# A fused mLSTM, attention and gated-mixing block on one Trainium2 core: norm factors and scales on GpSimd, and a load queue in emission order

## The chip, the cores and the metric

One core of a Trainium2 chip runs the whole block in one launch. The metric is device time in microseconds (us). The kernel before takes 1686.43 us, the median of three runs (1686.1 to 1689.79).

The profile's names for the engines are kept: PE is TensorE (matrix products), PEld its weight loads, ACT is ScalarE, DVE is VectorE, POOL is GpSimd, and SP is the engine whose queue issues most DMAs. Each engine works through its own list of instructions in order; semaphores make it wait for the others.

## The reference, cut to what matters

Sequence and width are 1024, all in float32.

```python
h = rmsnorm(x, norm_g)
(a_q, a_k, a_v, a_o, a_z, a_g, b_q, b_k, b_v, b_z, g_a, g_b) = split(h @ w_in)
# branch A: mLSTM, 4 heads of width 256, once forwards and once backwards in time
q, k = silu(depthwise_conv([a_q, a_k]))
h_fw, h_bw = mlstm(q, k, a_v, gates[0], gates[1]), flip(mlstm(flip(q), flip(k), ...))
hm  = rmsnorm(h_fw + h_bw, ml_norm_g)              # over the 256 of each head
y_a = hm * sigmoid(a_o) * silu(a_z)
# branch B: differential attention, 8 heads
y_b = rmsnorm(attention(b_q, b_k, b_v), da_subln_g) * 0.8 * silu(b_z)
# mixing
mix = sigmoid(g_a + gb[0]) * (y_a @ w_branch_a) + sigmoid(g_b + gb[1]) * (y_b @ w_branch_b)
x   = x + mix @ w_out
return rmsnorm(x, final_g)
```

## The kernel before

**Products.** Every float32 operand is split into a high and a low part (tile names end in H and L: `wH`, `wL`, `vH`, `sl_yb`), and a product is three matmuls: high by high, high by low, low by high. ACT makes the high part by a cast, and DVE or POOL the low part by a subtraction.

**Stages.** Projections and gates open the program; the attention of branch B runs to about 1120 us of the profiled span and stores y_b to DRAM; the mLSTM of branch A runs from there to about 1384 and stores y_a; the mixing runs to about 1591; the output product and the last norm end it. Projections of the gates g_a, g_b (`gate_units`) and of the next head's `v` are filled in between as spare work for PE.

**Order.** `build` puts small units of work into a list, in part interleaved by a `Weaver`, and `run` emits them. From the end of the opening on, the call `keep(E.PE)` makes PE execute in the order of emission. The instructions of ACT, DVE, POOL and SP are put in order by the framework's scheduler, from its own model of their times; on the chip this order is fixed.

**mLSTM head (`ml_head`).** A head has 8 blocks of 128 time steps, and a recurrent state for chunks of 256 in each direction. `weigh` scales the transposed k by its weights: `kwH` on ACT (L1081), then `kwL` on DVE (L1082); `kwH` has a single buffer, so the next half's copy waits for this half's `kwL`. `state` multiplies `vH` by `kwH` into a bank T (L127) and adds it to the state `C` (L1105). `split` casts the state to its parts CH and CL. `scores` (L1119 on) makes the decay weights `W`: POOL masks a row of gates with an affine select (L1136, once 128 and once 256 wide in a block), ACT takes the exponential (L1138), and DVE multiplies it by the scores SS and sums `den` (L1139). `t_tile` normalises: `den`, its reciprocal `rr`, and L1183 (ACT) and L1185 (DVE), which write the scaled `W`. `transposes` turns `W` on PE into a bank T, ACT and DVE split it (L1198, L1035), and `pv` multiplies it by v into PO. `pv` also adds the result to `hm` (L1209) and takes its square sum `ssq` (L1210).

**The head's norm.** After its last block, `pv` calls `rsqrt`: five short DVE operations on 128x8 (L140, L148 to L151) around one power on POOL (L147), with tiles `rh_v`, `rh_y`, `rh_w`. `scale` then multiplies the eight 128x256 tiles `hm` by `rh_y` on ACT (L1216). They are emitted among the first blocks of the *next* head. `load_g` brings the stored gates, and `out` transposes `hm` on PE (`T<-hm`), multiplies by `ml_norm_g` and the gates (L1228) and stores y_a. The last head has no next one: its scales and outputs are in `late`, woven with gate projections. The attention's norm calls the same `rsqrt` with `eng` set to POOL.

**Mixing.** `load_y` (L1310) loads a 512 KB block of y_b or y_a into one of two buffers `yraw`, casts it to its high part on ACT (L1314) and subtracts on DVE (L1315) for the low part; the parts lie in slots of the groups `yb` and `r`, the tiles `sl_yb` and `sl_r`. The y_b loads are woven with the last quarters of the gate projections (`rest`), whose results go from ACT's tanh (L837) through the one buffer `gt` to DRAM (L838, a DMA on SP's queue after the opening). `mix_units` runs pass B (`gb`: y_b by `w_branch_b`) and then pass A. For each block of 128 outputs it loads the gate (`tgl`, L1327) and a weight (`raw`, L173), PE multiplies into `pj`, which has two banks (L429), and DVE multiplies by the gate (L1339 in pass B), which frees the bank. The y_a blocks 0 to 3 are loaded during the second half of pass B, and 4 to 7 at its end.

Of the kernel before, what the change touches and what calls it, by code (L numbers as in the profile page):

```python
# [7 lines left out]
F32 = mybir.dt.float32  # L8
# [3 lines left out]
ALU = mybir.AluOpType  # L12
AX = mybir.AxisListType

S = 1024
D = 1024
EPS = 1e-6
NH_A, DH = 4, 256
NH_B = 8
L = 256  # L20
# [25 lines left out]
class Unit:  # L46
# [5 lines left out]
    def __init__(self, cost, fn, keys=(), tag=None, hold=0.0, name=None, after=(), lane=0):  # L52
        self.cost, self.fn, self.keys = cost, fn, keys
        self.tag, self.hold, self.name, self.after, self.lane = tag, hold, name, after, lane
# [55 lines left out]
class Block:  # L110
    def __init__(self, tc, A):
        self.tc, self.nc, self.A = tc, tc.nc, A
        nc = self.nc
        self.v, self.a, self.p, self.t, self.q = nc.vector, nc.scalar, nc.gpsimd, nc.tensor, nc.sync
        self.wt = {}
        self.raws = {}
        self.ml, self.opening, self.ahead, self.terms, self.forms = False, True, False, {}, 0
        self.rs, self.tk, self.loaded = {}, {}, set()
        for n in ("w1", "w2", "wy", "wr"):
            setattr(self, n, _Late(self, "_" + n))  # L120
        self.gc = {}
# [709 lines left out]
    def gate_units(self, seg, i):  # L831
        key = ("w_in", OFF[seg] + 128 * i)
        idx = (0 if seg == "ga" else 8) + i

        def done(half, ps):
            t = self.wpool.tile([128, 512], F32, name="gt", tag="gt")
            self.a.activation(out=t, in_=ps, func=AF.Tanh, scale=0.5, bias=self.gbh[:, idx:idx + 1])  # L837
            (self.a if self.opening else self.q).dma_start(out=self.tg[seg][i][:, half * 512:(half + 1) * 512], in_=t)  # L838
        return sum((self.proj(key, half, lambda ps, half=half: done(half, ps)) for half in range(2)), [])


# [186 lines left out]
    def ml_head(self, n, st):  # L1028


        v, a, p, q, w2 = self.v, self.a, self.p, self.q, self.w2
        gc = self.gc
        row = lambda c: n * NC + c
        loc = {}
# [167 lines left out]
        def pv(tt):  # L1202
            vH, vL = st["v", tt // NB]
            WH, WL = loc.pop(("WT", tt))
            pairs = [(x[:, i, :], y[:, i, 0:DH]) for x, y in ((WH, vH), (WH, vL), (WL, vH)) for i in range(NB)]
            o = self.bank("PO")[:, 0:DH]
            self.mm(o, pairs)
            h = st["h"][tt]
            v.tensor_tensor(out=h, in0=o, in1=h, op=ALU.add)  # L1209
            a.activation(out=o, in_=h, func=AF.Square, accum_out=st["ssq"][:, tt:tt + 1])  # L1210
            if tt == 7:
                loc["rs"] = self.rsqrt(w2, st["ssq"], 1.0 / DH, EPS, "rh")

        def scale(t):
            for t in (t, t + 1):
                a.mul(st["h"][t], st["h"][t], loc["rs"][:, t:t + 1])  # L1216

        def load_g(half):
            for i in range(2):
# [3 lines left out]
        def out(i, half):  # L1223
            ps = self.bank("T")
            for k in range(4):
# [5 lines left out]
        do = lambda f, *x: Unit(0.0, lambda: f(*x))  # L1231
        step = lambda f: lambda *x: [do(f, *x)]
        return dict(k=step(load_k), HL=lambda c: [do(load_parts, seg, c) for seg in ("ak", "aq")], gb=step(load_gb),
                    v=self.v_units("av", n, vv, order=(3, 2, 1, 0)), weigh=step(weigh),
                    state=lambda c, d: [do(state, c, d, i) for i in range(2)], split=step(split), S=step(scores),
                    I=step(t_tile), T=step(transposes), P=step(pv), scale=step(scale), g=step(load_g),
                    O=lambda half: [do(out, i, half) for i in range(2)])

# [68 lines left out]
        return un, prev["O"](0) + prev["g"](1) + prev["scale"](4) + prev["scale"](6) + prev["O"](1)  # L1307


    def load_y(self, src, i, slot):  # L1310
        raw = self.wy.tile([128, S], F32, name="yraw", tag="yraw", bufs=2)
        self.q.dma_start(out=raw, in_=src[i])
        h, l = slot("H"), slot("L")
        self.a.copy(h, raw)  # L1314
        self.v.tensor_tensor(out=l, in0=raw, in1=h.bitcast(F32), op=ALU.subtract)  # L1315
        return h, l

    def slot(self, which, dt=F32R):
        pool, bufs = {"yb": (self.wy, 16), "mb": (self.wy, 8), "r": (self.wr, 16)}[which]
        return pool.tile([128, S], dt, name="sl_" + which, tag=which, bufs=bufs)  # L1320
# [108 lines left out]
    def build(self):  # L1429
# [19 lines left out]
        do = lambda f, cost=0.0: Unit(cost, f)  # L1449
        pool = lambda *x, **k: tc.tile_pool(*x, **k)  # L1450
        with pool(name="const", bufs=1) as self.const, \
# [3 lines left out]
            E, kept = mybir.EngineType, []  # L1455

            def keep(*engines):

                def f():
                    if kept:  # L1460
                        kept.pop().__exit__(None, None, None)
                    if engines:
                        kept.append(tc.manual_schedule(engines=set(engines)))
                        kept[0].__enter__()
                return Unit(0.0, f)
# [18 lines left out]
            gq = [("gb", i) for i in range(8)] + [("ga", i) for i in range(8)]  # L1484
            fill = lambda m: sum((self.gate_units(*gq.pop(0)) for _ in range(m)), [])
# [16 lines left out]
            st3 = {}  # L1502
            w = Weaver()
            w.add(enter("h", "hpool"), enter("tab", "tab", side="right"), enter("tf", "tf", side="right"),
                  enter("p0", "p0", side="right"), banks("ps0", T=6), keep(E.PE, E.Activation, E.DVE, E.Pool), do(begin))
            k = self.PIECES
# [60 lines left out]
            w.add(enter("w2", "w2", side="right"), banks("ps2", T=2, SS=1, PO=1, I=1))  # L1567
            ml, late = self.ml_units([self.ml_head(n, stm[n]) for n in range(NH_A)], fill(2))
            w.add(do(lambda: setattr(self, "ml", True)), *ml)
            rest = fill(len(gq))  # L1570
            cut = len(rest) // 4
            w.add(*rest[:5])
            w.weave(late, rest[5:cut])
            w.add(do(lambda: setattr(self, "ml", False)), leave("ps2", "w2"), enter("wy", "wy", side="right"))
            yb = lambda x: self.slot("yb")
            loads = [do(lambda k=k: st3.__setitem__(("gb", k), self.load_y(self.yb, k, yb)), 1.0) for k in range(8)]
            w.weave(loads, rest[cut:])

            w.add(leave("h"), enter("wr", "wr"))
            passB = self.mix_units("gb", st3)  # L1580
# [1 line left out]
            loads = [do(lambda k=k: st3.__setitem__(("ga", k), self.load_y(self.ya, k, r)), 1.0) for k in range(4)]  # L1582
            w.add(*passB[:len(passB) // 2])
            w.weave(loads, passB[len(passB) // 2:])
            w.add(*[do(lambda k=k: st3.__setitem__(("ga", k), self.load_y(self.ya, k, yb))) for k in range(4, 8)])
            passA = self.mix_units("ga", st3)
            loads = [do(lambda k=k: self.load_wo(k, st3, "yb"), 1.0) for k in range(3)]
            k = len(passA) // 2
# [52 lines left out]
```

## Time and profile before

| | |
|---|---|
| median of three runs | 1686.43 us |
| the profiled execution's own time | 1687.36 us |
| its span in the profile | 1685.6 us |
| mean granted clock | 0.999 |

| stretch of the span, us | PE busy | ACT | DVE | POOL |
|---|---|---|---|---|
| 0 to 110, opening | 97.59 | 59.32 | 69.72 | 67.30 |
| 110 to 1120, projections and attention | 1004.36 | 479.80 | 644.88 | 456.63 |
| 1120 to 1384, mLSTM | 251.55 | 147.83 | 162.65 | 67.11 |
| 1384 to 1591, gates and mixing | 204.88 | 54.05 | 80.89 | 39.81 |
| 1591 to 1685.6, output | 87.37 | 19.33 | 34.22 | 4.35 |

The profile page gives one execution: how long each engine was busy, which waits it had and what ended them, and the DMAs. A wait is written as the waiting engine and its operation, then `<-` and the engine and operation that released it. An idle time of PE is the difference between a stretch and its busy time; in the mLSTM it is 264.0 - 251.55 = 12.5 us, in the mixing 207.0 - 204.88 = 2.1 us.

### The profile page before, as it was taken

How to read it: one execution, taken by the hardware profiler on the slowest of the kernel's cores; microseconds unless marked ns; L12 is line 12 of the kernel's file. 1: busy time of each engine (PE TensorE's matmuls, PEld its weight loads, DVE VectorE, ACT ScalarE, POOL GpSimd, SP SyncE). 2: the span in 40 equal slices, each digit the busy share in tenths (PEclk: the TensorE clock that was granted, in tenths of full speed). 3: DMA queues.
4: the chain of work that ended last, by engine and by line, in shares of the span. 5: the costliest groups of instructions: out<-in, count | busy, mean ns of one | idle time of the engine just before them, and what ended most of it. 6: DMA issues, size and time to landing. Idle time of an engine off the chain costs nothing. (4 is left out here: it accounts for less than half of the span.)

```text
span 1685.6 us, 25370 instructions
## 1 busy us (share of the span) xinstructions
PE 1645.8 (98%) x9431; PEld 1385.3 (82%) x9431; DVE 992.4 (59%) x1799; ACT 760.3 (45%) x1522; POOL 635.2 (38%) x712
## 2 busy tenths in 40 slices
PE   7999999999999999999999999999999999999998
PEld 5777887887877988898888888899999877888887
DVE  5778678675286766666666665325666754135533
ACT  7454555553255454444445445334655644122221
POOL 5767676655343334333451332122322412212000
PEclk9999999999999999999999999999999999999999
DMA  5334434434231213211322222166455337344222
GB/s 180 101 117 137 138 113 137 126 125 127 74 80 48 74 38 88 51 51 39 100 59 56 62 58 70 57 181 176 144 160 161 89 117 244 126 149 126 88 93 83
DMA packets 175630, 178.79 MB, mean 106 GB/s; under 512 B 12185, under 2 KB 135410, under 8 KB 175506
## 3 DMA queue, kind: packets, MB, share of 16 engines
q1 hardware_dynamic: 174594, 175.58, 34.8%
q8 instruction: 74, 1.21, 0.3%
q10 hardware_dynamic: 912, 1.59, 0.2%
q14 instruction: 50, 0.41, 0.1%
HBM read 114.11 MB, written 46.24 MB: 95 GB/s over the span
## 5 line engine op out<-in xcount | busy, mean ns | idle before, releaser
L429 PE MATMUL pj<-hH,wH 128*128 128x512 f32 x640 | 265.8, 415 | 3.3 <-ACT f L542 1.5
L429 PE MATMUL pj<-hH,wL 128*128 128x512 f32 x640 | 251.3, 393 | 1.8 <-POOL wL L207 1.8
L429 PE MATMUL pj<-hL,wH 128*128 128x512 f32 x640 | 250.1, 391 | 0.2 <-DVE hL L580 0.2
L209 POOL TENSOR_TENSOR wL<-raw,wH 128x1024 fp32r<-128x1024 f32 x41 | 99.7, 2432 | 278.0 <-ACT wH L204 268.3
L928 ACT ACTIVATE e<-S,nm 128x1024 f32<-128x1024 f32 x128 | 142.7, 1115 | 134.1 <-DVE nm L926 133.9
L948 DVE TENSOR_TENSOR pL<-T,pH 128x512 fp32r<-128x512 f32 x128 | 87.9, 688 | 117.4 <-ACT pH L947 116.7
L926 DVE TENSOR_REDUCE nm<-S 128x1 f32<-128x1024 f32 x128 | 150.5, 1217 | 10.1 <-PE S L923 9.3
L451 PE MATMUL pj<-wH,hH 128*128 128x256 f32 x512 | 149.9, 293 | 1.6 <-DVE vL L1035 1.4
L429 PEld LDWEIGHTS pj<-hH,wH 128*128 128x128 f32 x640 | 120.4, 188 | 37.7 <-issue 14.1
L451 PE MATMUL pj<-wL,hH 128*128 128x256 f32 x512 | 144.9, 283 | 1.4 <-POOL wL L207 1.4
L429 PEld LDWEIGHTS pj<-hH,wL 128*128 128x128 f32 x640 | 120.1, 188 | 30.2 <-POOL wL L207 3.4
L451 PE MATMUL pj<-wH,hL 128*128 128x256 f32 x512 | 144.5, 282 | 0.0
L429 PEld LDWEIGHTS pj<-hL,wH 128*128 128x128 f32 x640 | 120.7, 189 | 18.2 <-DVE hL L580 0.6
L429 PE MATMUL pj<-sl_yb,wH 128*128 128x512 f32 x384 | 118.9, 390 | 2.1 <-DVE sl_mb L1339 1.6
L947 ACT CAST pH<-T 128x512 fp32r<-128x512 f32 x128 | 74.7, 584 | 100.5 <-PE T L131 99.8
L204 ACT CAST wH<-raw 128x1024 fp32r<-128x1024 f32 x56 | 58.8, 1050 | 114.7 <-PE pj L429 75.8
L923 PE MATMUL S<-kst,qq 64*128 64x512 f32 x768 | 106.5, 408 | 0.0
L451 PEld LDWEIGHTS pj<-wH,hH 128*128 128x128 f32 x512 | 97.7, 191 | 6.8 <-issue 3.9
L451 PEld LDWEIGHTS pj<-wL,hH 128*128 128x128 f32 x512 | 97.5, 190 | 2.3 <-POOL wL L207 2.3
L451 PEld LDWEIGHTS pj<-wH,hL 128*128 128x128 f32 x512 | 97.7, 191 | 0.1
L934 DVE SCALAR_TENSOR_TENSOR e<-e,r,e 128x1024 f32<-128x1024 f32 x64 | 88.9, 1389 | 2.2
L923 PEld LDWEIGHTS S<-kst,qq 64*128 64x128 f32 x768 | 67.8, 184 | 26.2 <-issue 10.5
(358 smaller groups left out, 4101.4 us busy)
## 6 DMA issues: line engine op xcount, KB each, us to landing
raw<-in_w_in_dram SPq DMA_DIRECT2D x88, 512.0 KB, 3.9
kst<-hl SPq DMA_DIRECT2D x64, 128.0 KB, 2.4
qq<-hl SPq DMA_DIRECT2D x64, 128.0 KB, 2.4
x<-in_x_dram SPq DMA_DIRECT2D x8, 512.0 KB, 6.2
cak<-y SPq DMA_DIRECT2D x16, 256.0 KB, 2.3
cakH<-cin SPq DMA_DIRECT2D x16, 256.0 KB, 4.4
cakL<-tz SPq DMA_DIRECT2D x16, 256.0 KB, 4.1
gm<-oz SPq DMA_DIRECT2D x16, 256.0 KB, 2.8
```

The lines of the kernel that those rows point to most:

```text
L204: self.a.copy(wH, raw)
L209: self.p.tensor_tensor(out=wL, in0=raw, in1=wHf, op=ALU.subtract)
L429: self.t.matmul(ps, lhsT=l[:, k, :], rhs=r, start=(n == 0), stop=(n == 23))
L451: self.t.matmul(ps[:, i, :], lhsT=l, rhs=r[:, k, :], start=(kh == 0 and k == 0 and m == 0), stop=(kh == 1 and k == 3 and m == 2))
L923: self.t.matmul(ps[:, o], lhsT=qq[r, x, c], rhs=k[r, y, o], start=(m == 0), stop=(m == 2))
L926: v.tensor_reduce(out=nm, in_=ps, axis=AX.X, op=ALU.max, negate=True)
L928: a.activation(out=e, in_=ps, func=AF.Exp, bias=nm[:, 0:1], accum_out=Z[:, j, t:t + 1])
L934: v.scalar_tensor_tensor(out=e0, in0=e, scalar=r[:, 0:1], in1=e0, op0=ALU.mult, op1=ALU.add)
L947: a.copy(pH[:, :, s], ps)
L948: v.tensor_tensor(out=pL[:, :, s], in0=ps, in1=pH[:, :, s].bitcast(F32), op=ALU.subtract)
```

## The change

It has two parts.

*The mLSTM's norm.* All of `rsqrt` for a head goes to POOL (`eng=p`). The eight scales of heads 0 to 2 become `tensor_scalar` multiplications on POOL; those of the last head stay on ACT. Nothing else of the head is edited.

```diff
             if tt == 7:
-                loc["rs"] = self.rsqrt(w2, st["ssq"], 1.0 / DH, EPS, "rh")
+                loc["rs"] = self.rsqrt(w2, st["ssq"], 1.0 / DH, EPS, "rh", eng=p)
 
         def scale(t):
             for t in (t, t + 1):
-                a.mul(st["h"][t], st["h"][t], loc["rs"][:, t:t + 1])
+                if n + 1 < NH_A:
+                    p.tensor_scalar(out=st["h"][t], in0=st["h"][t], scalar1=loc["rs"][:, t:t + 1], scalar2=None, op0=ALU.mult)
+                else:
+                    a.mul(st["h"][t], st["h"][t], loc["rs"][:, t:t + 1])
```

*The queue and the loads.* From the mixing on, SP too keeps the order of emission. The eight y_b loads are emitted ahead of the last gate projections instead of being woven with them. `load_y` by default loads straight into the slot of the low part, and the subtraction is done in place; y_a's blocks 4 to 7 keep the way through `yraw`. The stores of the gates go to ACT's DMA queue from a flag `last` on, which a unit at the head of `rest` sets; since `rest` is one unit longer, `rest[:5]` holds one piece of a gate projection fewer ahead of `late`.

```diff
-            (self.a if self.opening else self.q).dma_start(out=self.tg[seg][i][:, half * 512:(half + 1) * 512], in_=t)
+            (self.a if self.opening or self.last else self.q).dma_start(out=self.tg[seg][i][:, half * 512:(half + 1) * 512], in_=t)
...
-    def load_y(self, src, i, slot):
-        raw = self.wy.tile([128, S], F32, name="yraw", tag="yraw", bufs=2)
-        self.q.dma_start(out=raw, in_=src[i])
-        h, l = slot("H"), slot("L")
+    def load_y(self, src, i, slot, direct=True):
+
+        if direct:
+            h, l = slot("H"), slot("L")
+            raw = l.bitcast(F32)
+            self.q.dma_start(out=raw, in_=src[i])
+        else:
+            raw = self.wy.tile([128, S], F32, name="yraw", tag="yraw", bufs=2)
+            self.q.dma_start(out=raw, in_=src[i])
+            h, l = slot("H"), slot("L")
...
-            rest = fill(len(gq))
+            rest = [do(lambda: setattr(self, "last", True))] + fill(len(gq))
...
-            w.weave(loads, rest[cut:])
+            w.add(keep(E.PE, E.SP), *loads, *rest[cut:])
...
-            w.add(*[do(lambda k=k: st3.__setitem__(("ga", k), self.load_y(self.ya, k, yb))) for k in range(4, 8)])
+            w.add(*[do(lambda k=k: st3.__setitem__(("ga", k), self.load_y(self.ya, k, yb, False))) for k in range(4, 8)])
```

Behind the edits the line numbers are larger by 3 (L1216 is L1219 for ACT's scale and L1217 for POOL's, L1228 is L1231) and by 9 from `slot` on (L1314, L1315, L1327 and L1339 are L1323, L1324, L1336 and L1348); a direct load is at L1318. PE's list is the same but for three products, which move behind the last head's transpositions of `hm`.

The scheduler moves more than the edits say. POOL's list at the first change of heads, where head 0's norm meets head 1's first blocks; `-` is before, `+` the change, and the numbers in tile names only tell buffers apart:

```order
 L1136 AFFINE_SELECT W_12377<-gb 128x128
+L140 TENSOR_SCALAR rh_v<-ssq 128x8
 L147 TENSOR_TENSOR rh_y<-rh_v,mhalf 128x8
+L148 TENSOR_TENSOR rh_w<-rh_y 128x8
+L149 TENSOR_TENSOR rh_w<-rh_w,rh_v 128x8
+L150 TENSOR_SCALAR rh_w<-rh_w 128x8
+L151 TENSOR_TENSOR rh_y<-rh_y,rh_w 128x8
+L1217 TENSOR_SCALAR hm<-hm,rh_y 128x256 x7
 L1136 AFFINE_SELECT W_12383<-gb 128x256
+L1217 TENSOR_SCALAR hm<-hm,rh_y 128x256
```

The five DVE operations of the norm and seven of the eight scales now stand between the block's two selects.

ACT's list at the same place, with the exponentials of those two selects (L1138):

```order
 L1179 ACTIVATE hm<-I,al 128x256
 L1138 ACTIVATE W_12377<-W_12377,gc_negM 128x128
-L1216 ACTIVATE hm<-hm,rh_y 128x256 x3
-L1198 CAST WH<-T 128x256
-L1081 ACTIVATE kwH<-T,gc_ws 128x256
+L1198 CAST WH<-T 128x256
 L1138 ACTIVATE W_12383<-W_12383,gc_negM 128x256
-L1216 ACTIVATE hm<-hm,rh_y 128x256
-L1081 ACTIVATE kwH<-T,gc_ws 128x256
-L1060 CAST vH<-pj 128x2x256
-L1216 ACTIVATE hm<-hm,rh_y 128x256
+L1081 ACTIVATE kwH<-T,gc_ws 128x256 x2
```

The scales leave ACT, and the first copy to `kwH`, which stood ahead of the wide exponential, now stands behind it.

DVE's list at the start of pass B, from the last head's outputs on, before:

```order
L1228 SCALAR_TENSOR_TENSOR gA<-T,mlg,gA 128x512 x4
L1315 TENSOR_TENSOR sl_yb<-yraw,sl_yb 128x1024 x8
L1315 TENSOR_TENSOR sl_r<-yraw,sl_r 128x1024 x2
L1339 SCALAR_TENSOR_TENSOR sl_mb<-tgl,pj 128x512
L1315 TENSOR_TENSOR sl_r<-yraw,sl_r 128x1024 x2
L1339 SCALAR_TENSOR_TENSOR sl_mb<-tgl,pj 128x512 x14
```

and with the change:

```order
L1231 SCALAR_TENSOR_TENSOR gA<-T,mlg,gA 128x512 x4
L1324 TENSOR_TENSOR sl_yb<-sl_yb 128x1024 x8
L1348 SCALAR_TENSOR_TENSOR sl_mb<-tgl,pj 128x512 x5
L1324 TENSOR_TENSOR sl_r<-sl_r 128x1024
L1348 SCALAR_TENSOR_TENSOR sl_mb<-tgl,pj 128x512 x2
L1324 TENSOR_TENSOR sl_r<-sl_r 128x1024
```

y_a's first subtraction stood ahead of the first operation that frees PE's bank, and now stands behind five of these.

More of the change, by code (lines that the diff above doesn't have):

```diff
@@ L117, in __init__ @@
         self.ml, self.opening, self.ahead, self.terms, self.forms = False, True, False, {}, 0
-        self.rs, self.tk, self.loaded = {}, {}, set()
+        self.rs, self.tk, self.loaded, self.last = {}, {}, set(), False
         for n in ("w1", "w2", "wy", "wr"):
```

## The prediction

> **What bounds the kernel now.** I read the page's busy shares first, then PE's waits stage by stage, then the timeline at the few places that hold them. Engines go by the page's names: PE is TensorE, ACT ScalarE, DVE VectorE, POOL GpSimd, SP the queue that issues most DMAs.
>
> ```profile
> span 1685.6 us, 25370 instructions
> PE 1645.8 (98%) x9431; PEld 1385.3 (82%) x9431; DVE 992.4 (59%) x1799; ACT 760.3 (45%) x1522; POOL 635.2 (38%) x712
> ```
>
> PE is busy for 98% of the span, so an edit can only fill or widen PE's gaps. PE's list of waits, for the mLSTM (1130 to 1390 us; two lines that the change doesn't touch left out) and for the mixing (1390 to 1600): what waited, for whom, us in total, times, longest.
>
> ```profile
> PE T L131 <- ACT W L1183: 3.4, 5, 0.8
> PE T L131 <- DVE W L1185: 2.7, 3, 1.8
> PE T L131 <- ACT hm L1216: 1.0, 2, 0.5
> PE PO L127 <- ACT WH L1198: 0.7, 3, 0.3
> PE T L127 <- ACT kwH L1081: 0.4, 2, 0.2
> ```
>
> and in the mixing:
>
> ```profile
> PE pj L429 <- DVE sl_mb L1339: 1.6, 1, 1.6
> PE pj L429 <- DVE sl_yb L1315: 0.4, 2, 0.2
> ```
>
> The change can win some 8 us at most in the first and 2 in the second. ACT and DVE have room, so work taken off them pays only where PE waits for them.
>
> **First change of heads (head 0's norm beside head 1's first tiles).** These rows, of PE, ACT, DVE and POOL in turn, are start, duration, engine, line, tiles.
>
> ```profile
> 1212.93 0.28 PE L127 MATMUL T<-vH,kwH 128*128 128x258 f32 x1
> 1215.11 0.28 PE L127 MATMUL SS<-akH,aqH 128*128 128x256 f32 x1
> 1217.44 0.72 PE L131 MATMUL T<-ident,W 128*128 128x128 f32 x2 [0.75 <-ACT W L1183]
> 1217.91 0.36 PE L451 MATMUL pj<-wH,hH 128*128 128x256 f32 x1
> 1207.12 0.19 ACT L1210 ACTIVATION_READ_ACCUMULATOR PO<-hm 128x1 f32 x1
> 1211.96 0.47 ACT L1081 ACTIVATE kwH<-T,gc_ws 128x256 fp32r<-128x256 f32 x1
> 1212.33 0.50 ACT L1138 ACTIVATE W<-W,gc_negM 128x256 f32<-128x256 f32 x1
> 1213.62 0.48 DVE L1082 SCALAR_TENSOR_TENSOR kwL<-T,gc_ws,kwH 128x256 fp32r<-128x256 f32 x1 [0.68 <-ACT kwH L1081]
> 1217.42 0.35 DVE L1185 SCALAR_TENSOR_TENSOR W<-W,rr,W 128x128 f32<-128x128 f32 x1
> 1207.37 0.29 POOL L1136 TENSOR_SCALAR_AFFINE_SELECT W<-gb 128x128 f32<-128x128 f32 x1 [1.05 <-DVE W L1185]
> 1209.43 0.40 POOL L1136 TENSOR_SCALAR_AFFINE_SELECT W<-gb 128x256 f32<-128x256 f32 x1
> ```
>
> Removed: five small DVE operations and eight ACT scales. Moved: in the new order the 256-wide select stands on POOL behind the whole norm chain and seven scales. The exponential that reads it (L1138) stands on ACT ahead of both kwH copies, so it becomes a wait; behind it queue kwH, vH and CH, and PE's state product waits for kwH. The chain's price is that of the attention's norm, which runs on POOL already:
>
> ```profile
> 624.87 1.68 POOL L147 TENSOR_TENSOR rb_y<-rb_v,mhalf 128x8 f32<-128x8 f32 x1
> 627.48 0.20 POOL L151 TENSOR_TENSOR rb_y<-rb_y,rb_w 128x8 f32<-128x8 f32 x1
> 627.77 0.23 POOL L978 TENSOR_SCALAR rb_y<-rb_y 128x8 f32<-128x8 f32 x1
> ```
>
> From the power to the end of L151 is 627.68 - 624.87 = 2.81 us. No row shows a 128x256 TENSOR_SCALAR on POOL; its price lies between the same operation on 128x8 (0.20 to 0.23 us; more elements can't be shorter) and the two-input operation, 0.50 for 128x128 and 1.29 for 128x512, so about 0.76 for 128x256:
>
> ```profile
> L207 POOL TENSOR_TENSOR wL<-raw,wH 128x128 fp32r<-128x128 f32 x120 | 55.2, 496 | 35.3 <-ACT wH L204 33.2 <-POOL W L1136 2.0
> L865 POOL TENSOR_TENSOR m<-m,hl 128x512 f32<-128x512 f32 x16 | 20.6, 1288 | 66.1 <-DVE hl L863 66.1
> ```
>
> I take 0.42, just above the undisturbed select of the same size and one input (0.40 at 1209.43); 0.20 and 0.76 stay as ends.
>
> The Trainium skill, GPSIMD Engine Reference, section 4.1 (Engine selection), speaks against this part: for elementwise work on a tile it names VectorE, since GpSimd is about half as fast with two inputs and near line rate with one. By its section 3.1, 2.6 cycles an element at 1.2 GHz gives an estimate of 0.55 + 0.2 = 0.75 us a scale and a sum 6 us higher; 1.03 cycles gives 0.42 and this sum. The trace has both rates, not this operation.
>
> Now the sum. POOL's first select ends at 1207.66 and the last square sum is there at 1207.31. The first norm operation (0.23 and a gap of 0.08) starts at 1207.7, the power at 1208.0, L151 ends at 1210.8, seven scales (2.9) at 1213.8, the select at 1214.2. ACT's next operation followed the exponential by 0.40 before, so kwH starts at 1214.65, 2.7 later than 1211.96. Then kwH, kwL, kwH come one after the other (each half's kwL reads what the next kwH overwrites), 0.47 + 0.48 + 0.46 + 3 x 0.05, and the second kwL starts at 1216.2, 2.6 later than 1213.62. PE came to the scores (SS) 1.5 us after it, so at 1217.7, and would be at the transposition of W 1.4 later, 1219.1. But DVE's L1185 came 3.8 us after that kwL, and what stands between them still adds up to some 3.7 us: 1219.9 + 0.35, and PE goes on at 1220.4 instead of 1217.91. **+2.5 us**, with today's waits for WH (0.3) and W (0.75) already spent in it. The second change of heads has the same rows 61.5 us later: **+2.5**.
>
> **Third change of heads.** Here POOL gets three scales ahead of the narrow select and one more ahead of the wide one.
>
> ```profile
> 1331.44 0.44 PE L131 MATMUL T<-ident,W 128*128 128x128 f32 x2 [1.80 <-DVE W L1185]
> 1335.97 0.28 PE L127 MATMUL SS<-akH,aqH 128*128 128x256 f32 x1
> 1329.09 1.64 POOL L147 TENSOR_TENSOR rh_y<-rh_v,mhalf 128x8 f32<-128x8 f32 x1
> 1331.46 0.29 POOL L1136 TENSOR_SCALAR_AFFINE_SELECT W<-gb 128x128 f32<-128x128 f32 x1 [0.74 <-DVE rh_w L150]
> 1334.50 0.47 DVE L1082 SCALAR_TENSOR_TENSOR kwL<-T,gc_ws,kwH 128x256 fp32r<-128x256 f32 x1
> ```
>
> The 1.80 us wait goes, since DVE no longer stands still for the power. What is late next is kwH: the chain ends at 1332.1, three scales at 1333.4, the narrow select at 1333.75, its exponential lets kwH start at 1334.1, the second kwL at 1335.6 instead of 1334.50. The scores come 1.1 later, the next W 0.2 more: **+1.3 us** net.
>
> **Last head.** Its scales stay on ACT, its chain goes to POOL, and three products (0.68 us) slip behind the transpositions of hm.
>
> ```profile
> 1380.12 3.31 ACT L1216 ACTIVATE hm<-hm,rh_y 128x256 f32<-128x256 f32 x8 [1.91 <-DVE rh_y L151]
> ```
>
> The sum of squares is there at 1376.46, so the chain ends at 1379.63 and the scales start 0.44 earlier; they are what PE waits for, so 0.68 - 0.44 = **+0.2 us**.
>
> **Mixing.** yb goes straight into the slot of its low part, SP issues in emission order, and six gate stores go to ACT's queue.
>
> ```profile
> 1423.69 0.61 PE L429 MATMUL pj<-sl_yb,wH 128*128 128x512 f32 x2
> 1424.14 0.39 PE L429 MATMUL pj<-sl_yb,wL 128*128 128x512 f32 x1
> 1426.14 0.73 PE L429 MATMUL pj<-sl_yb,wH 128*128 128x512 f32 x2 [1.61 <-DVE sl_mb L1339]
> 1431.48 0.39 PE L429 MATMUL pj<-sl_yb,wL 128*128 128x512 f32 x1
> 1431.99 0.50 PE L429 MATMUL pj<-sl_yb,wH 128*128 128x512 f32 x1
> 1424.26 1.23 DVE L1315 TENSOR_TENSOR sl_r<-yraw,sl_r 128x1024 fp32r<-128x1024 f32 x1 [2.38 <-ACT sl_r L1314]
> 1425.40 0.68 DVE L1339 SCALAR_TENSOR_TENSOR sl_mb<-tgl,pj 128x512 f32<-128x512 f32 x1
> yraw<-yb SPq DMA_DIRECT2D x8, 512.0 KB, 4.1
> tgb<-gt ACTq DMA_DIRECT2D x6, 256.0 KB, 2.0
> ```
>
> DVE subtracts ya's low part in front of the L1339 that frees PE's bank. In the new order five L1339 stand ahead of the first of these. PE steps (1424.14 - 1423.69)/2 = 0.23 us a product, so the gaps are 1426.14 - 1424.37 = 1.8 and, at the next half, 1431.99 - 1431.71 = 0.3; both go: **-2.0 us**. The eight loads, even at 4.1 us one by one, are 33 us, from 1387 to 1420; overlapped they end near 1405, and PE wants yb's first at 1413.5, its eighth at 1418. Weight 1 queues behind them and is wanted at 1424: covered with some 10 us to spare. A gate store lands 2.0 us after issue on ACT's queue, under the 5.4 us between gates. Uncovered, one late load would cost up to its 4 us.
>
> **Sum:** 2.5 + 2.5 + 1.3 + 0.2 - 2.0 = +4.5 us. The profiled execution itself took 1687.36 us, 1.76 outside the span, and would take 1691.9; the median of the three runs is 1686.43, so I predict **1690.9 us**.
>
> **Rivals.** (a) *One-input scales at about 0.42 us*, as summed. 7 + 7 + 4 = 18 scales stand in front of kwH. The sum passes 0.2% (3.4 us, about what a measurement of this kernel can tell from no change) from 0.36 us a scale on: chance 0.64, of it 0.12 within the bound. (b) *Two-input price*, 0.76: 18 x 0.34 = 6.1 more, 1697.0; for it the two-input rows, against it the select. Chance 0.07. (c) *The mixing turns against it*: ACT issues stores between gates and casts, SP stands in line behind them. Instead of -2.0 a transfer of 4 us lies open: 1690.9 + 6 = 1697. The spans above speak against it; 0.06. (d) *Scales near 0.20, or the delay is taken up by later slack*: +0.5 down to the mixing's -2.0 alone, 1687 to 1684.4, within 0.2%. Against it: PE has hardly a wait later in a head to give back. 0.17. (e) *Faster*: in the changes of heads kwH is not held up, because the wide select still lands in time. Then PE loses only today's waits: two times some 1.3 (0.3, 0.2 and 0.75), 1.5 of the 1.80, and the mixing's 2.0, in all -6.1: 1680. PE took its first state product at 1212.93, and 0.3 earlier without its wait for WH; for that the select must end by about 1211.7. The chain alone ends at 1210.8, so seven scales and the select would have 0.9 us, under 0.1 each. 0.06.
>
> **Chances and range.** Slower 0.52 + 0.07 + 0.06 = 0.65, same 0.12 + 0.17 = 0.29, faster 0.06. The range goes from (d)'s 1684 to 1697, the high end of the price.
>
> **What would show it.** Right: a PE wait "T L127 <- ACT kwH" of some 2.5 us at two changes of heads and over 1 at the third; POOL's seven L1217 scales back to back at 0.4 us; no wait for L1348 (before: L1339) in the mixing. Wrong: kwH copies before the exponential's wait ends, scales far from 0.42, PE waiting for ACT's gates or for yb.

## The result and the profile after

The changed kernel takes 1704.39 us (median of 4 runs, 1703.22 to 1705.77), beside 1688.11 us for the kernel before: a ratio of 1.0098, 95% interval [1.0085, 1.011]. The profiled executions took 1703.22 and 1687.36 us, 15.9 us apart. Forecast were +4.5 us and a range up to 1697: the sign was right, the size wrong.

The head of the page after (span, then busy time of each engine):

```profile
span 1701.4 us, 25379 instructions
PE 1650.0 (97%) x9431; PEld 1390.8 (82%) x9431; DVE 987.2 (58%) x1779; ACT 753.1 (44%) x1498; POOL 659.4 (39%) x756
```

PE does the same work; what is new is waiting. PE's waits in the mLSTM (1130 to 1400 us), then in the mixing: who waited for whom, us in total, times, longest.

```profile
PE T L127 <- ACT kwH L1081: 12.5, 3, 6.0
PE T L127 <- POOL hm L1217: 3.2, 1, 3.2
PE T L131 <- ACT W L1183: 1.9, 3, 0.7
PE T L131 <- DVE W L1185: 1.2, 3, 0.5
```

```profile
PE pj L429 <- DVE sl_yb L1324: 1.0, 2, 0.8
```

The first fence holds the mLSTM, the second the mixing's main one. The waits of before for W shrank (3.4 to 1.9 and 2.7 to 1.2), and so did the mixing's (2.0 to 1.2 with one of 0.2 for the cast), but the wait for kwH went from 0.4 to 12.5 us. The 3.2 us put down to `hm` L1217 belong to it too: they are the third change's wait. The product that ends it reads vH and kwH and not `hm`; kwH is there at 1347.69 + 0.46 = 1348.15, and a scale that ends between that and the product's start is named in its place.

```profile
1347.69 0.46 ACT L1081 ACTIVATE kwH<-T,gc_ws 128x256 fp32r<-128x256 f32 x1
1348.29 0.36 PE L127 MATMUL T<-vH,kwH 128*128 128x258 f32 x1 [3.17 <-POOL hm L1217]
```

The first change of heads after, in POOL's, ACT's and PE's rows (start, duration, engine, line, tiles):

```profile
1210.95 0.20 POOL L151 TENSOR_TENSOR rh_y<-rh_y,rh_w 128x8 f32<-128x8 f32 x1
1211.26 6.35 POOL L1217 TENSOR_SCALAR hm<-hm,rh_y 128x256 f32<-128x256 f32 x7
1217.56 0.40 POOL L1136 TENSOR_SCALAR_AFFINE_SELECT W<-gb 128x256 f32<-128x256 f32 x1
1217.99 0.51 ACT L1138 ACTIVATE W<-W,gc_negM 128x256 f32<-128x256 f32 x1 [8.01 <-POOL W L1136]
1218.41 0.46 ACT L1081 ACTIVATE kwH<-T,gc_ws 128x256 fp32r<-128x256 f32 x1
1218.92 0.58 PE L127 MATMUL T<-vH,kwH 128*128 128x258 f32 x1 [6.03 <-ACT kwH L1081]
```

This is the forecast chain link by link: norm chain, seven scales, select, exponential, kwH, state product. The norm ends at 1211.15 (forecast 1210.8; this execution comes to the place 0.34 us later than before's), but a scale takes 6.35 / 7 = 0.91 us, not 0.42, so kwH starts at 1218.41 and not at 1214.65.

The long wait has a companion, the granted clock (windows: busy time of PE, PEld, DVE, ACT and POOL, the clock, DMA share, GB/s):

```profile
1215.00:1216.00 1.00, 0.00 (x0) 0.00 (x0) 0.00 (x0) 0.00 (x0) 1.00 (x2) 0.99 0.18 63
1216.00:1217.00 1.00, 0.00 (x0) 0.00 (x0) 0.00 (x0) 0.00 (x0) 1.00 (x2) 0.50 0.00 0
1221.00:1222.00 1.00, 1.00 (x7) 1.00 (x6) 1.00 (x5) 0.37 (x2) 0.00 (x0) 0.50 0.00 0
1222.00:1223.00 1.00, 1.00 (x7) 1.00 (x7) 1.00 (x6) 0.92 (x4) 0.00 (x0) 0.60 0.00 0
1223.00:1224.00 1.00, 1.00 (x11) 1.00 (x10) 1.00 (x6) 1.00 (x4) 0.26 (x1) 1.00 0.00 0
```

Some 3 us into the wait the clock halves, and stays so for 3.8 us of work behind it. At the second change it halves 4.2 us into the wait and stays so for 5.0 us of work. Whether that is a loss of its own had to be tried. (The Trainium skill, TensorE: Matmul & The Clock Gate, Part 1, gives half the clock after an idle window of about 3.4 us; at these two waits the trace is near it, with 3.1 and 4.2 us.) The rows at 1215 and 1216 show one thing more: nothing but POOL works there, so a scale takes 0.91 us with no other engine in its way.

### The profile page after: what moved, and what is told of

Read it like the earlier page. It is cut to its first block, busy times and chain, and to the rows that moved or that the text cites. A ratio compares the mean times of both kernels' runs of the same rounds, so it can differ in the third digit from the quotient of the medians.

```text
span 1701.4 us, 25379 instructions
## 1 busy us (share of the span) xinstructions
PE 1650.0 (97%) x9431; PEld 1390.8 (82%) x9431; DVE 987.2 (58%) x1779; ACT 753.1 (44%) x1498; POOL 659.4 (39%) x756
```

## The experiments

PE works in a fixed order, so a change of heads can be measured inside one profile, by the time between starts of PE's transpositions of W around it. First and second change are one such interval, the third is three.

| run | 1st, us | 2nd, us | 3rd, us | ratio to before [95%] |
|---|---|---|---|---|
| before | 8.59 | 8.54 | 21.64 | 1 |
| the change | 14.68 | 15.16 | 25.89 | 1.0098 [1.0085, 1.011] |
| mix_only | 8.58 | 8.55 | 21.68 | 1.0 [0.9991, 1.0009] |
| norm_only | 15.53 | 15.54 | 26.17 | 1.0107 [1.0092, 1.0122] |
| chain_only | 8.97 | 8.93 | 23.81 | 1.001 [1.0001, 1.0019] |
| four_scales | 11.84 | 12.04 | 27.43 | 1.007 [1.0053, 1.0087] |
| two_ops | 11.75 | 12.00 | 24.63 | 1.0044 [1.003, 1.0058] |

**mix_only: which part.** `rsqrt` without `eng=p`, all scales on ACT.

> The changed kernel with the mLSTM's norm and scales put back as they were before; only the mixing part (queue order, direct loads, gate stores on ACT's queue) is new. Theory P (price and place: each scale on POOL takes 0.91 us and seven of them stand ahead of the select that the exponential and then kwH wait for): the mixing part has no share in the loss and the time is 0.5 to 2 us below before; PE's 1.6 us wait for L1339 (now L1348) is gone. Rival M (the mixing part costs, by loads that come late or stores that hold ACT): 2 us or more above before, with PE waits for yb's parts of over 2 us.

1688.83 us beside 1688.38: no difference; by the interval at most 1.5 of the 0.5 to 2 us that were expected can be there. The wait for L1339 is gone, as said. From the last head's second group of transpositions to the output's first product PE takes 207.5 us (1383.49 to 1591.03) instead of 207.7 (1383.15 to 1590.86) and does the three moved products (0.7 us) besides; but as these no longer stand ahead of the transpositions, PE waits 1.2 us for the first `hm` in place of 0.5. In this execution the clock is also halved right behind that, while PE works:

```profile
1384.00:1386.00 2.00, 2.00 (x10) 1.80 (x9) 1.39 (x3) 0.00 (x0) 0.00 (x0) 0.50 0.71 262
```

PE needs 3.9 us from the second group to its seventh product behind it, where before it needed 2.45 at full clock. So some 1.5 us of the mixing's gain are covered by this stretch of half clock; whether the longer wait for `hm` brings it about, no run shows. Rival M falls.

**norm_only: the other part.** The kernel before with the first diff alone.

> The kernel before with the norm chain on POOL and three heads' scales on POOL; the mixing is as before. Theory P: the whole loss and some more, 16 to 18 us above before, PE's wait for kwH 6.0 us at two changes of heads. Rival M: under 13 us above before, since the mixing part carries the rest.

1706.88 us, 18.5 above before: the whole loss. The run shows something else as well. In the mLSTM the lists of PE, ACT, DVE and POOL are the same as with the whole change, and PE's wait at the first change is the same (6.05 and 6.03 us), yet the interval is 0.85 us longer. What differs is the clock: here it is still halved up to 1225.0, 6.0 us behind the wait's end at 1219.03 and not 3.8.

```profile
1223.00:1225.00 2.00, 2.00 (x11) 2.00 (x11) 2.00 (x8) 1.52 (x4) 0.30 (x1) 0.50 0.03 8
1224.81 0.47 PE L131 MATMUL T<-ident,W 128*128 128x128 f32 x2
```

W is ready at 1223.77, and PE comes to it 1.0 us late, without a wait; in the changed run it is 0.2 us late at the first change and 0.7 at the second.

**chain_only: chain or scales.** The change with `a.mul` for all heads.

> The changed kernel with all scales on ACT again; the norm chain stays on POOL. Theory P: the chain alone ends at about 1210.9 and the wide select near 1211.3, before ACT comes to its exponential, so the loss goes: from 0 to 3 us below before. Rival C (it is the 2.8 us chain on POOL, ahead of the select, that holds kwH): 5 us or more above before, PE's wait for kwH still 2 us or more.

1690.19 us, about 1.8 above, where 0 to 3 below were expected. The first two changes are 0.4 us from before, so the chain does not hold kwH there; rival C falls. The third is still 2.2 us longer than before, against the expectation: two scales of ACT now wait for the chain ahead of the cast of WH (rows of ACT and PE), and the clock is halved from 1337.4 to 1340.8, while PE works without a wait (one window, columns as in the first window table).

```profile
1333.56 0.91 ACT L1216 ACTIVATE hm<-hm,rh_y 128x256 f32<-128x256 f32 x2 [2.61 <-POOL rh_y L151]
1334.77 0.50 PE L127 MATMUL PO<-vH,WH 128*128 128x256 f32 x2 [1.09 <-ACT WH L1198]
```

```profile
1338.00:1340.00 2.00, 2.00 (x11) 2.00 (x11) 1.22 (x5) 2.00 (x7) 0.30 (x1) 0.50 0.00 0
```

**four_scales: the number of scales.**

```diff
-                if n + 1 < NH_A:
+                if n + 1 < NH_A and t >= 4:
```

> The changed kernel with the scales of blocks 0 to 3 of each head on ACT and 4 to 7 on POOL: four scales stand ahead of the wide select at the first two changes of heads, and at the third POOL has none ahead of the selects. Theory P: 3 x 0.91 = 2.7 us less wait at each of the first two changes (6.0 to about 3.3), the third change's 4.2 us gone, so about +6 us against before (4 to 8). Rival C: hardly a change, +12 us or more. Rival K (a large part of the loss is the halved clock after PE's long wait, not the wait): the wait of 3.3 us is too short for the clock to fall, and the time is below +4 us.

1699.87 us, 11.5 above: outside the band of 4 to 8. The first two changes did what theory P says: three scales fewer are 2.8 and 3.1 us less (3 x 0.91 = 2.7). The third was misread: its four POOL scales kept their place ahead of the selects, and ACT's four wait for the chain as in chain_only, so both delays add up. Rival K isn't tested here: the clock was halved for 3.4 us at the first two changes and for 6.8 us at the third all the same.

**price: the scale itself.**

```diff
...
+                    if n == 0:
+                        p.tensor_tensor(out=h, in0=h, in1=r.to_broadcast([128, DH]), op=ALU.mult)
+                    elif n == 1:
+                        p.tensor_scalar(out=h, in0=h, scalar1=0.5, scalar2=None, op0=ALU.mult)
+                    elif t % 2:
+                        p.tensor_scalar(out=h, in0=h, scalar1=r, scalar2=1.0, op0=ALU.mult, op1=ALU.mult)
...
```

> The changed kernel with three forms of the scale on POOL: head 0 multiplies two tensors (the norm factor broadcast along the row), head 1 multiplies by the constant 0.5 (its own factors are left out), head 2 has odd blocks with a second operation (times 1.0) behind the factor and even blocks as in the change. Theory S (reading the factor of each partition is what costs): the constant takes 0.40 to 0.45 us, the broadcast 0.76, the rest 0.91. Theory F (every 128x256 TENSOR_SCALAR on POOL is that slow): constant and factor both 0.9, the broadcast 0.76. Theory N (a second operation costs by itself): odd blocks of head 2 are longer than even ones by 0.2 us or more.

The run leaves out head 1's factors, so only its durations are read. The groups of POOL, by form (count, total, mean ns): broadcast, constant, factor alone, factor and a second operation.

```profile
L1219 POOL TENSOR_TENSOR hm<-hm,rh_y 128x256 f32<-128x256 f32 x8 | 4.7, 615 | 0.1
L1221 POOL TENSOR_SCALAR hm<-hm 128x256 f32<-128x256 f32 x8 | 6.9, 860 | 16.5 <-ACT PO L1210 16.4
L1225 POOL TENSOR_SCALAR hm<-hm,rh_y 128x256 f32<-128x256 f32 x4 | 3.7, 927 | 0.1
L1223 POOL TENSOR_SCALAR hm<-hm,rh_y 128x256 f32<-128x256 f32 x4 | 2.0, 496 | 0.0
```

Theories S and N fall: the constant is nearly as slow as the factor, and the second operation makes it *faster*, 0.50 against 0.93 us. F holds only for the form with one operation. The two-input form (0.615) is faster than the one-input form of the change.

**two_ops: the price alone, at the same place.**

```diff
-... scalar2=None, op0=ALU.mult)
+... scalar2=1.0, op0=ALU.mult, op1=ALU.mult)
```

> The changed kernel with one edit: the scale on POOL gets a second operation (times 1.0) behind the factor, and nothing moves in any queue. Theory P (price and place) with the 0.48 us that this form took for head 2's odd blocks: seven scales take 3.4 us in place of 6.35, PE's wait for kwH falls from 6.0 to about 3.0 at the first two changes of heads, the third is shorter by 4 x 0.43 = 1.7, and the time is about 8 us above before (6 to 10). Rival H (the short form was only fast between two long ones, or the price isn't what sets the loss): 13 us or more above before.

```profile
1213.86 3.21 POOL L1217 TENSOR_SCALAR hm<-hm,rh_y 128x256 f32<-128x256 f32 x7
1218.38 0.39 PE L127 MATMUL T<-vH,kwH 128*128 128x258 f32 x1 [2.90 <-ACT kwH L1081]
```

1696.24 us, 7.4 above before. The wait falls from 6.03 to 2.90, by what seven scales are cheaper (6.35 - 3.21 = 3.14). The lists of PE, ACT, DVE and POOL are unchanged, so more than half of the loss was the form of one instruction.

**fill_pe: the clock.**

```diff
+            if n and (c, d, i) == (0, 0, 0):
+                x = st["aq", 0][0]
+                self.mm(ps[:, 0:DH + 2], [(x[:, j % 2, 0:128], vH[:, j // 2 % 2, :]) for j in range(20 if n == 3 else 40)])
             self.mm(ps[:, 0:DH + 2], pairs)
```

> The changed kernel with products into the state's bank that nobody reads, put on PE ahead of the first state product after each change of heads: 40 (4.8 us) at the first two, 20 (2.4 us) at the third. They lie inside PE's wait for kwH and keep the clock up. Theory P (the wait sets the loss, and the slow stretch after it lies beside the chain of ACT and DVE from kwH to W): the clock stays at 1.00, and each change of heads is shorter by 0 to 0.5 us, 1.5 us in all at most. Rival K (the halved clock after the wait is a loss of its own): 1.4 us or more less at each change, over 4 us in all.

```profile
1219.00:1221.00 2.00, 1.40 (x5) 0.78 (x5) 1.02 (x4) 1.45 (x5) 0.41 (x1) 1.00 0.00 0
1221.00:1223.00 2.00, 2.00 (x16) 2.00 (x17) 1.97 (x8) 1.08 (x4) 0.00 (x0) 1.00 0.00 0
```

At the first change the clock stays at 1.00, and the interval is 14.50 us, 0.18 shorter: rival K's 1.4 us are not there. The whole run (1705.66 us, one execution) is no faster. But it isn't a clean comparison. At the second change the clock still fell. The scheduler also moved ACT's and DVE's lists behind each change: L1185 now stands ahead of DVE's copies to `C`, PE waits 0.7 us ahead of the first transposition of W, which the profile puts to such a copy, and the next interval is 0.8 us longer. So the run does not give the clock's price alone. norm_only gives it better, and leaves the half clock as a small loss of its own, 0.2 to 1.0 us at a change by how late PE comes to W, beside a wait of 6 us.

**late_kept: the place.** The norm becomes a unit of its own behind block 2's selects, scales and outputs follow one block later, and POOL keeps the order of emission at the changes.

```diff
+                if prev and t == 0:
+                    un.append(self.keep(mybir.EngineType.PE, mybir.EngineType.Pool))
+                if prev and t == 5:
+                    un.append(self.keep(mybir.EngineType.PE))
...
+                if prev and t == 1:
+                    un += prev["norm"]()
+                if prev and t in (2, 3):
+                    un += prev["scale"](4 * t - 8) + prev["scale"](4 * t - 6)
```

> The changed kernel with the same work on POOL, but its order kept by hand at the changes of heads: the norm is emitted behind the selects of block 2, the scales behind those of blocks 3 and 4 (four each), the outputs one block later than before. Theory P (it is the place in POOL's queue): the selects come in time, PE's wait for kwH is under 0.5 us at each change though every scale still takes 0.9 us, and the time is 1 to 5 us below before, since the waits for W of before (0.75, 0.75, 1.8) go too. Rival L (POOL's load or what it shares with DVE slows the head): 5 us or more above before.

1683.12 us, ratio 0.9968 [0.9956, 0.998], though each scale still takes 0.9 us: no wait for kwH is left. Rival L's 5 us above before do not come. But what it names shows once, at the third change, where PE waits 5.3 us for W in the profiled execution:

```profile
1330.87 3.67 POOL L1219 TENSOR_SCALAR hm<-hm,rh_y 128x256 f32<-128x256 f32 x4
1334.51 6.66 POOL L207 TENSOR_TENSOR wL<-raw,wH 128x128 fp32r<-128x128 f32 x16
1335.18 6.14 DVE L1185 SCALAR_TENSOR_TENSOR W<-W,rr,W 128x128 f32<-128x128 f32 x1
1341.38 0.69 PE L131 MATMUL T<-ident,W 128*128 128x128 f32 x2 [5.35 <-DVE W L1185]
```

The operation that PE waits for is DVE's L1185. It takes 6.14 us where it otherwise takes 0.35, and it ends 0.15 us after the last of 16 subtractions that POOL runs back to back for two weights. DVE looks held while POOL works; the rows show that the two end together, not why. No select of POOL is in the way, since the next one starts only behind L1185. The profiled execution is the slowest of six (1686.39 us, the fastest 1682.04), so the others may not have this wait.

**best3: both together.** The late norm for heads 0 and 1 only, with two operations; head 2 as before; the mixing as changed.

> The mixing part as changed; the norm and scales of heads 0 and 1 late and in POOL's order by hand as in the run with the late norm, with the scale of two operations; head 2's norm and scales on DVE and ACT at the places of before. Theory P: the two first changes of heads are about 3 us shorter than before each, the third is as before, and the time is 5 to 9 us below before. Rival L2 (the gain of the late norm came from the third change or from chance): within 2 us of before.

1681.3 us, ratio 0.9955 [0.9941, 0.9968], 7.6 us below before and the fastest kernel here. The stretch of six intervals around the first change takes 45.61 us (before 48.56) and around the second 45.61 (48.58). The first of these as a window, in this run:

```profile
1202.06:1247.67 45.61, 45.12 (x374) 44.13 (x373) 31.74 (x114) 24.77 (x62) 15.35 (x42) 1.00 0.55 167
```

and before:

```profile
1200.56:1249.12 48.56, 46.30 (x374) 44.47 (x373) 32.46 (x119) 27.59 (x70) 11.43 (x29) 1.00 0.55 158
```

The same 374 matmuls, and PE idle for 0.5 us in place of 2.3. Against rival L2, 5.9 of the 7.6 us lie around the first two changes.

**flag_apart: the shifted cut.** mix_only with the flag set by a unit outside `rest`.

> The mixing part alone, with the flag for the stores set by a unit of its own, so that the gate projections around the last head are cut as before (three products back ahead of the transpositions of hm). If the shifted cut is what eats the mixing's gain, PE's first wait for hm is 0.5 us again (1.17 with the shifted cut) and the output product begins 0.5 to 1 us earlier against the same head's end; if not, nothing moves.

The wait for hm is 0.51 us again, but in the mixing PE waits 1.0 us for `sl_yb`, 0.5 for its cast and 0.2 for a gate. From the first transposition of hm to the output 209.8 us pass (mix_only 210.0, before 210.2). It moved 0.2 us against mix_only, where 0.5 to 1 were expected, in a single execution of 1690.2 us. The waits in the mixing are 1.3 us longer here than in mix_only, and mix_only has its stretch of half clock, so the run does not settle what the shifted cut costs.

## Why the prediction was wrong

- **First and second change of heads (forecast +2.5 each).** The mechanism was right, and one factor failed: "I take 0.42, just above the undisturbed select of the same size and one input". It is 0.91. With 7 x (0.91 - 0.42) = 3.4 more the step gives +5.9; measured, with the next interval, which gives 0.35 back, are +5.7 and +6.3. The second has the same wait as the first and 0.5 us more behind it, where the clock stays halved 1.2 us longer; the forecast had no term for the clock. two_ops, at 0.46 to 0.48, has +3.2 and +3.5 (2.8 and 3.1 with the next interval), where the step at 0.48 gives +2.9.
- **The upper bound.** "So about 0.76 for 128x256", from two-input rows, was no bound: it rests on the belief that one input can't cost more than two. In this form it does. The 18 scales ahead of kwH make 18 x 0.49 = 8.8 us, most of the 11.3 us by which the forecast (+4.5) misses the measured 15.8 between spans.
- **The rule of the Trainium skill** (GPSIMD Engine Reference, section 4.1) pointed the right way, against elementwise work on GpSimd. The estimate of 0.75 us a scale from section 3.1, and 6 us more, were still short of the 0.91 us measured. That one input runs near line rate, as section 4.1 says, does not hold for this form: 0.86 to 0.93 us with one input, 0.615 with two.
- **Third change (+1.3).** The 1.80 us wait for W went, as said, and kwH came late, as said. With four scales 0.49 dearer the step gives +3.3; measured +4.25. Behind the last wait PE runs at half clock (1349.1 to 1352.5) and reaches the next transposition of W 0.8 us after W is ready, without a wait: that would be the rest, but at this change it is argued from the rows, not shown.
- **Last head and mixing (+0.2 and -2.0).** Together -1.0 from the end of the third change to the output. Up to the second group of transpositions of `hm` PE takes 37.5 us in place of 37.9, with the three products (0.7) still to do: +0.3. The rest is then -1.2. The two gaps at L1339 are gone, as said. y_a's low part, through `yraw`, has waits of 1.2 us where before had 0.4, which is about what is missing; mix_only, with the same lists in the mixing, has 0.4 again, so these waits change from one execution to the next. Loads of y_b and gate stores were covered, and rival (c) did not come.
- **What is left** of the 15.8 us, some 0.5, lies ahead of the first change and behind the output's first product, where nothing was edited.
- **Rival (e)** would have come about with another order: late_kept shows that the select in time wins, even at 0.9 us a scale.

## What to carry to other kernels

Moving work to an idle engine puts it into that engine's queue: look at what stands behind it there, and who waits for that. An operation of which the trace has no row needs its price measured in its exact form before it goes ahead of something that is waited for; a related form is no bound. A long run of work on one engine can also go with a long wait on another, as with POOL and DVE in late_kept. Where a scheduler places it, its model of the price decides the order, so the place has to be held by hand when the model may be off.

## What the runs showed of the hardware

- On GpSimd a 128x256 float32 TENSOR_SCALAR with one multiplication takes 0.86 us with a constant and 0.91 to 0.93 with a factor for each partition; with a second multiplication behind it 0.48 to 0.50; a TENSOR_TENSOR with the factor broadcast 0.615.
- The granted clock halves for about 3.4 us (1349.1 to 1352.5; chain_only 1337.4 to 1340.8) or multiples of it (6.8 us, 1216.0 to 1222.8; norm_only 10.2 us, 1283.0 to 1293.2). One long wait is not needed: in chain_only the longest waits of PE in the 5 us ahead were 1.1 and 0.3 us, and PE was busy for 3.6 of the 5.
- An operation of DVE can last until POOL is done. In late_kept L1185 took 6.14 us beside 0.35, up to the end of a run of POOL's subtractions. In the kernel before, a 128x512 operation of DVE (L1345, from 1527.89) took 2.11 us beside 0.69, while POOL was in a subtraction of 2.72 us that ended at 1529.45. Which operations are held in this way, no run here settles.
